# A hybrid decoder block on one core: how the front of its mixers empties its banks, shifts by one token and scales its rows

## The chip, the cores and the metric

One Trainium2 chip; the kernel runs on one of its cores. The metric is the device time of one execution in microseconds (us). Five engines work side by side, each through its own queue of instructions in a fixed order: TensorE (PE in the profile, PEld its weight loads), VectorE (DVE), ScalarE (ACT), GpSimd (POOL) and SyncE (SP), which here only issues DMAs. "ACTq" in a row is a DMA that ACT issues.

## The reference

One decoder layer over 512 tokens of width 1024, all in float32. It has four parts, of which the change touches the first:

```
u = rms_norm(h, norm_mix_g)
z = u @ w_in                                   # 1024 x 3328
o_da = diff_attention(z[:, :1536], ...)        # q, k, v of 512 columns each
o_rw = rwkv7_mix(z[:, 1536:], ...)             # r, k, v of 512 columns, 256 of lora
h = h + concat([o_da, o_rw]) @ w_out
h = h + peer_ffn(rms_norm(h, norm_ffn_g), ...)
h = h + sigmoid(rms_norm(h, norm_ple_g) @ ple_gate_w) * (p @ ple_proj_w)
return rms_norm(h, norm_final_g)
```

And of `rwkv7_mix`, what comes ahead of its recurrence:

```
prev = pad(z_rw[:, :-1], one row of zeros ahead)     # the row of the token before
zs = z_rw + (prev - z_rw) * mu
r, k, v, xw, xa, xg = split(zs)
w = -softplus(-(w0 + tanh(xw) @ w_up)) - 0.5
a = sigmoid(a0 + xa @ a_up);  g = sigmoid(xg) @ g_up
kk = k * k_k;  k = k * (1 + (a - 1) * k_a)
kk = kk / max(norm of kk in each head, 1e-12)
...
y = y + sum(r * k * r_k, over a head) * v
```

The recurrence is computed in chunks of 32 tokens, which needs the keys and the update directions multiplied by running products of the decay and by their inverses.

## The kernel before

Tokens stand on the 128 partitions in four blocks b of 128. Each float32 matmul is done as three in a rounded format: an operand is split into a high half (`hi`, a copy on ACT, L128) and a low half (`lo`, the rest, on DVE, L134), and hi x hi, hi x lo and lo x hi are added in the same bank (L200 to L202). A projection (`proj_steps`, L190) goes over eight k-steps of 128 input columns; in each it does 4 token blocks x 3 matmuls into four banks `acc`, and after the eighth step each block's `consume` empties its bank. The weights arrive by `fetch` on SP in pairs of k-steps (`wraw`, three buffers) and are split with the norm's gain as a scale into `whi` and `wlo`, two buffers of a pair each.

`mixers` (L804) does the front of the two mixers in this order:

- The input's transposed columns `xT` are split pair by pair (`columns`, L830) inside the first projection. The row scales, one over the root mean square of each token, are not applied to the input but to each bank when it is copied out.
- Four projections for the RWKV side, of 512 columns each but for lora's 256: "k", "l" (lora), "r", "v". Their `consume` (in `shift_group`, L403) copies the bank on ACT with the row scale `rs` (L414), then issues two or three DMAs on ACT that write the same tile one row further down (L417, L418, L422: the shift by one token), and then mixes on POOL with three instructions (L423, L424, L426).
- The row scales: POOL squares the columns of `xT` and adds them up (L838, L840, L842), PE adds over partitions with a column of ones (`row_scales`, L847) at k-step 7 of the key group, ACT takes the root (L118), DVE the reciprocal.
- After "r", `rw_keys` (L430) normalises the keys of all four blocks: products on DVE, squares on ACT, a root by Newton steps of small DVE instructions (`rsqrt`, L85).
- `rope_tables` (L319) and `lambdas` (L303) are small work on DVE with Sin and Exp on ACT (L389, L395, L313).
- Then, for each block, `rw_prepare` (L445): tanh and sigmoid of lora's tile on ACT, small matmuls, prefix sums of the decay in each chunk (`pcum` L473, `prem` L480, `ppc` L484), their exponentials (`e_in`, `e_inv`, `e_ex`, `e_end`), the decayed tensors, sixteen transposes (`ptr`, L520), and the products of keys with keys inside a chunk (`psA`, L538). Of the decayed tensors POOL made `bon` (L494, L495), `bh` and `kh` (L504, L505), DVE the others: `aa` x `kk` (L501), and in place `aa` x `e_inv` and `k2` x `e_inv` (L509, L510), which the transposes read.
- Between the steps of `rw_prepare` stand steps of the three projections for attention (q, k, v), of the rope and its transposes (`da_prepare`, L717), as `WEAVE` says, and steps of a small triangular solve (`rw_solve`) in block 2, as `PACE` says.

What follows is not touched: the recurrence and the attention, the out-projection, and then the retrieval with its large streams of weights, which is most of the span.

The order on each engine in this part is not that of the code alone. A scheduler of the framework lists the instructions by its own costs and priorities, pools set when a buffer comes free (`p2` has 28 tiles of 128x512, `p4` 14 of 128x1024), and `behind(i, first)` puts an instruction after another one on its engine without a semaphore. The retrieval's loop and the tail have an order written by hand.

Of the kernel before, what the change touches and what calls it, by code (L numbers as in the profile page):

```python
# [8 lines left out]
F32 = mybir.dt.float32  # L9
# [4 lines left out]
AF = mybir.ActivationFunctionType  # L14
# [39 lines left out]
class Kernel:  # L54
# [248 lines left out]
    def lambdas(self, pool):  # L303
# [9 lines left out]
        nc.scalar.activation(e, e, AF.Exp)  # L313
# [5 lines left out]
    def rope_tables(self, pool, tmp):  # L319
# [69 lines left out]
        nc.scalar.activation(self.sin.rearrange("p b j -> p (b j)"), x0, AF.Sin)  # L389
# [7 lines left out]
    def p2(self, name, shape=(128, 512), dt=F32):  # L397
        return self.pages.tile(list(shape), dt, name=name, tag="p2", bufs=28)
# [4 lines left out]
    def shift_group(self, rs, alloc, g0, n):  # L403
# [7 lines left out]
        def consume(b, ps):  # L411
            z = self.p2("z")
            zt[b] = z
            nc.scalar.activation(z[:, :n], ps, AF.Copy, scale=rs[:, b:b + 1])  # L414
            zp = self.p2("zp")

            nc.scalar.dma_start(zp[1:113, :n], z[0:112, :n])  # L417
            nc.scalar.dma_start(zp[113:128, :n], z[112:127, :n])  # L418
            if b == 0:
                nc.vector.memset(zp[0:1, :n], 0.0)  # L420
            else:
                nc.scalar.dma_start(zp[0:1, :n], zt[b - 1][127:128, :n])  # L422
# [22 lines left out]
    def rw_prepare(self, b, psum, r, k, v, kk, lx, st):  # L445
# [46 lines left out]

        bon = p2("bon")
        nc.gpsimd.tensor_tensor(bon, r, k2, op=OP.mult)  # L494
        nc.gpsimd.tensor_tensor(bon, bon, self.r_k, op=OP.mult)  # L495
        st["bonus"] = sm.tile([128, 8], F32, name="bonus", bufs=NB)
# [6 lines left out]
        bh, kh = p2("bh"), p2("kh")  # L503
        nc.gpsimd.tensor_tensor(bh, aa, e_end, op=OP.mult)  # L504
        nc.gpsimd.tensor_tensor(kh, k2, e_end, op=OP.mult)  # L505
        nc.sync.dma_start(by_row(self.d_bh[b]), bh)
        nc.sync.dma_start(by_row(self.d_kh[b]), kh)
        be, kt = aa, k2
        nc.vector.tensor_mul(be, aa, e_inv)  # L509
        nc.vector.tensor_mul(kt, k2, e_inv)  # L510
# [293 lines left out]
    def mixers(self, ocat_pool, psum):  # L804
# [3 lines left out]
        with ExitStack() as ctx:  # L808
# [17 lines left out]
            ones = cpool.tile([128, 1], F32, name="ones")  # L826
            nc.vector.memset(ones, 1.0)
            xs = {}

            def columns(k):  # L830

                xs[k] = self.p4("xt", [128, 2, T])
                nc.sync.dma_start(xs[k], a["xT"][k * 128:(k + 2) * 128, :].rearrange("(k p) t -> p k t", k=2))
                self.split(hi[:, k:k + 2], lo[:, k:k + 2], xs[k])

            def square(k):
                sq = xs[k]
                nc.gpsimd.tensor_tensor(sq, sq, sq, op=OP.mult)  # L838
                if k:
                    nc.gpsimd.tensor_tensor(xs[0], xs[0], sq, op=OP.add)  # L840
                if k == KC - 2:
                    nc.gpsimd.tensor_tensor(xs[0][:, 0], xs[0][:, 0], xs[0][:, 1], op=OP.add)  # L842

            def row_scales():
                ps = psum.tile([128, NB], F32, name="pss", tag="tp")
                for b in range(NB):
                    nc.tensor.matmul(ps[:, b:b + 1], xs[0][:, 0, b * 128:b * 128 + 128], ones, start=True, stop=True)  # L847
                self.rms(rs, ps)
# [4 lines left out]
            begin = {0: [lambda: columns(2), lambda: square(0)], 2: [lambda: columns(4), lambda: square(2)],  # L853
                     4: [lambda: columns(6), lambda: square(4)], 5: [lambda: square(6)],
                     6: [lambda: self.mixer_consts(cpool)], 7: [row_scales]}
            for tag, c0, n in (("k", 512, 512), ("l", 1536, 256), ("r", 0, 512), ("v", 1024, 512)):
# [6 lines left out]
                if tag == "r":  # L863
                    kks = [self.rw_keys(zs["k"][b]) for b in range(NB)]
# [27 lines left out]
            for b in range(NB):  # L892
                for i, _ in enumerate(self.rw_prepare(b, psum, zs["r"][b], zs["k"][b], zs["v"][b], kks[b], zs["l"][b],
                                                      sts[b])):
# [707 lines left out]
```

## Time and profile before

| | us |
|---|---|
| three runs | 1864.88, 1874.73, 1876.71 |
| their median | 1874.73 |
| the profiled execution | 1859.81 |
| its span in the profile | 1857.4 |

The profile is of one execution: its span runs from the first recorded instruction to the last, and 2.4 us lie around it. Its granted TensorE clock was 0.966 of full speed on the mean. Over the whole span PE was busy 1728.6 us (93%), DVE 1448.7 (78%), ACT 739.5 (40%) and POOL 653.0 (35%). A row of a timeline gives the start of an instruction, its duration, the engine, the line, the operation with the tiles that it writes and reads, and in brackets how long the engine had been idle and what ended that. Buffer numbers are left out of the tiles' names.

### The profile page before, as it was taken

To read this page: it belongs to the slowest core of one execution; us is meant where nothing else is said; L and a number is where in the kernel's file an instruction comes from. 1 tells how busy PE (TensorE), PEld (TensorE's weight loads), DVE (VectorE), ACT (ScalarE), POOL (GpSimd) and SP (SyncE) were. 2 spreads that over 40 slices of the span, in tenths; PEclk is the share of its full clock that TensorE was granted. 3 is DMA by queue.
4 is the path that set the end of the run, shared out by engine and by line. 5 is a ranking of instruction groups with operands and counts; after the bars stand their busy time and mean duration, and the time that the engine had idled before them with its cause. 6 is when DMAs were issued, how large, how long until landed. Compare 5 with 4: busy or idle time off the path is not lost.

```text
span 1857.4 us, 28657 instructions
## 1 busy us (share of the span) xinstructions
PE 1728.6 (93%) x10434; PEld 1465.3 (79%) x10434; DVE 1448.7 (78%) x3233; ACT 739.5 (40%) x1371; POOL 653.0 (35%) x447
## 2 busy tenths in 40 slices
PE   6887987897998987999999999999999999999998
PEld 5755665666777787998777788889899999989886
DVE  6476587667459999987888787887878787878786
ACT  3424342332335654444443433333333333333354
POOL 6662121110126664001111133334545555555530
PEclk9988997889999998999999999999999999999999
DMA  5533224441442343445665678777989898989891
GB/s 171 154 95 97 81 83 91 100 118 34 150 145 83 109 129 100 140 142 192 208 203 201 195 240 272 237 265 274 310 308 310 308 310 305 311 308 313 303 329 65
DMA packets 149842, 361.62 MB, mean 195 GB/s; under 512 B 43859, under 2 KB 58447, under 8 KB 149573
## 3 DMA queue, kind: packets, MB, share of 16 engines
q1 hardware_dynamic: 109924, 221.89, 37.2%
q0 software_dynamic: 36864, 134.23, 21.3%
q10 hardware_dynamic: 2912, 3.67, 0.7%
q8 instruction: 82, 1.34, 0.3%
q14 instruction: 60, 0.48, 0.1%
HBM read 330.51 MB, written 21.36 MB: 189 GB/s over the span
## 4 chain that ended last, share of the span: by engine, by line
PE 68%; DVE 22%; issue 4%; ACT 3%; DMA 1%; POOL 1%; ACTq 0%; SPq 0%; DVEq 0%; POOLq 0%
PE po L1270 21%; PE phid L1134 8%; PE phid L1136 8%; PE phid L1135 8%; PE pg L1239 2%; DVE wlo L132 2%; ACT whi L128 2%; PE acc L201 2%; DVE ids L1083 2%; PE acc L202 2%; PE acc L200 2%; DVE wlo L134 1%; PE psA L538 1%; DVE rest L977 1%; DVE jj L1227 1%
## 5 line engine op out<-in xcount | busy, mean ns | idle before, releaser
L132 DVE TENSOR_TENSOR wlo<-wraw,whi 128x1024 fp32r<-128x1024 f32 x243 | 297.6, 1225 | 150.5 <-ACT whi L128 150.4
L128 ACT ACTIVATE whi<-wraw 128x1024 fp32r<-128x1024 f32 x276 | 291.4, 1057 | 177.7 <-PE phid L1135 59.0
L1136 PE MATMUL phid<-u2dhi,wlo 128*128 128x384 f32 x1024 | 347.7, 340 | 12.7 <-POOL wlo L132 12.7
L1134 PE MATMUL phid<-u2dhi,whi 128*128 128x384 f32 x1024 | 350.9, 343 | 1.0 <-ACT row L1143 1.0
L1135 PE MATMUL phid<-u2dlo,whi 128*128 128x384 f32 x1024 | 346.9, 339 | 0.0
L1293 POOL DMA_INDIRECT row<-in_peer_u_dram,idx x128 | 190.7, 1490 | 404.5 <-DVE row L1305 222.2
L1293 POOL DMA_INDIRECT row<-in_peer_v_dram,idx x128 | 186.1, 1454 | 276.8 <-DVE h L1309 194.8
L1270 PE MATMUL po<-whi,chi 128*128 128x512 f32 x768 | 243.9, 399 | 1.2 <-ACT row L1143 1.2
L1270 PE MATMUL po<-whi,clo 128*128 128x512 f32 x768 | 243.1, 398 | 1.5
L1270 PE MATMUL po<-wlo,chi 128*128 128x512 f32 x768 | 241.4, 395 | 0.0
L1136 PEld LDWEIGHTS phid<-u2dhi,wlo 128*128 128x128 f32 x1024 | 194.7, 190 | 14.8 <-POOL wlo L132 14.8
L1134 PEld LDWEIGHTS phid<-u2dhi,whi 128*128 128x128 f32 x1024 | 194.8, 190 | 5.8 <-ACT row L1143 1.3
L1135 PEld LDWEIGHTS phid<-u2dlo,whi 128*128 128x128 f32 x1024 | 194.4, 190 | 3.7
L1270 PEld LDWEIGHTS po<-whi,clo 128*128 128x128 f32 x768 | 143.0, 188 | 42.0 <-DVE clo L134 8.7
L1270 PEld LDWEIGHTS po<-wlo,chi 128*128 128x128 f32 x768 | 144.4, 188 | 34.3
L1309 DVE SCALAR_TENSOR_TENSOR h<-row,ids,h 128x1024 f32<-128x1024 f32 x128 | 164.0, 1281 | 1.5
L128 ACT ACTIVATE chi<-gelu 128x384 fp32r<-128x384 f32 x128 | 67.4, 526 | 239.8 <-DVE gelu L1247 121.5
L1270 PEld LDWEIGHTS po<-whi,chi 128*128 128x128 f32 x768 | 141.1, 188 | 25.5 <-ACT row L1143 1.5
L1305 DVE SCALAR_TENSOR_TENSOR row<-row,xn 128x1024 f32<-128x1024 f32 x128 | 153.8, 1220 | 0.0
L1143 ACT ACTIVATE gelu<-phid 128x384 f32<-128x384 f32 x86 | 42.3, 492 | 266.9 <-PE phid L1136 266.9
L200 PE MATMUL acc<-whi,uhi 128*128 128x512 f32 (+1 forms) x224 | 91.1, 416 | 18.8 <-ACT whi L128 11.6
L132 POOL TENSOR_TENSOR wlo<-wraw,whi 128x1024 fp32r<-128x1024 f32 x33 | 78.8, 2400 | 68.9 <-ACT whi L128 68.9
(436 smaller groups left out, 2938.0 us busy)
## 6 DMA issues: line engine op xcount, KB each, us to landing
wraw<-in_peer_uT_dram SPq DMA_DIRECT2D x128, 512.0 KB, 3.9
wraw<-in_peer_v_dram SPq DMA_DIRECT2D x128, 512.0 KB, 6.2
wraw<-in_w_in_dram SPq DMA_DIRECT2D x24, 512.0 KB, 6.1
wraw<-in_peer_w_q_dram SPq DMA_DIRECT2D x16, 512.0 KB, 4.4
ahead<-row SPq DMA_DIRECT2D x42, 192.0 KB, 2.3
gelu<-ahead SPq DMA_DIRECT2D x42, 192.0 KB, 3.8
wraw<-in_w_out_dram SPq DMA_DIRECT2D x8, 512.0 KB
zp<-z ACTq DMA_DIRECT2D x12, 224.0 KB, 2.7
```

The costliest lines, as they stand in the source:

```text
L128: self.last_hi = nc.scalar.activation(hi, src, AF.Copy, **({} if g is None else {"scale": g}))
L132: self.last_lo = eng.tensor_tensor(lo, src, hi.bitcast(F32), op=OP.subtract)
L200: nc.tensor.matmul(o, hi[:, k, s], whi, start=(k == 0), stop=False)
L201: nc.tensor.matmul(o, hi[:, k, s], wlo, start=False, stop=False)
L1134: nc.tensor.matmul(ps, whi[:, s], hi[:, k, :], start=(k == 0), stop=False)
L1135: nc.tensor.matmul(ps, whi[:, s], lo[:, k, :], start=False, stop=False)
L1136: nc.tensor.matmul(ps, wlo[:, s], hi[:, k, :], start=False, stop=(k == KC - 1))
L1143: nc.scalar.activation(g, ps, AF.Gelu)
L1270: nc.tensor.matmul(outs[b, e], lhs[:, s], rhs[:, 512 * e:512 * e + 512], start=(c == 0 and rhs is vhi and lhs is chi), stop=(c == NKEY - 1 ...
L1293: nc.gpsimd.indirect_dma_start(out=row, out_offset=None, in_=a["peer_u" if kind == "U" else "peer_v"], in_offset=bass.IndirectOffsetOnAxis ...
L1305: nc.vector.scalar_tensor_tensor(row, row, 1.0, xn0, op0=OP.mult, op1=OP.mult, accum_out=hid0[:, k:k + 1])
L1309: nc.vector.scalar_tensor_tensor(acc0, row, hid0[:, k:k + 1], acc0, op0=OP.mult, op1=OP.add)
```

## The change

The change is in the front of the mixers alone, and its parts are these:

- A projection's four banks are emptied by four copies in a row, and only then come the shifts of the four blocks. The shifts' DMAs are issued by SP instead of ACT.
- The row scales are made from `x` itself: four loads of 128x1024 on SP, and for each a Square on ACT with its sum over the row (`squares`, L111). The squares on POOL and the small matmul on PE are gone.
- Exp of the lambdas and the first Sin are put behind the last bank copy that was issued (`last_z`).
- The keys are normalised block by block, ahead of each `rw_prepare`, instead of all after "r".
- `bon`, `bh` and `kh` are made on DVE instead of POOL, after `be` and `kt`, which now have tiles of their own; the other products go in place.

```diff
 def lambdas
-        nc.scalar.activation(e, e, AF.Exp)
+        self.behind(nc.scalar.activation(e, e, AF.Exp), self.last_z)
 def rope_tables
-        nc.scalar.activation(self.sin.rearrange("p b j -> p (b j)"), x0, AF.Sin)
+        self.behind(nc.scalar.activation(self.sin.rearrange("p b j -> p (b j)"), x0, AF.Sin), self.last_z)
 def shift_group
         def consume(b, ps):
-            z = self.p2("z")
-            zt[b] = z
-            nc.scalar.activation(z[:, :n], ps, AF.Copy, scale=rs[:, b:b + 1])
-            zp = self.p2("zp")
-
-            nc.scalar.dma_start(zp[1:113, :n], z[0:112, :n])
-            nc.scalar.dma_start(zp[113:128, :n], z[112:127, :n])
+            zt[b] = self.p2("z")
+            self.last_z = nc.scalar.activation(zt[b][:, :n], ps, AF.Copy, scale=rs[:, b:b + 1])
+            if b == NB - 1:
+
+                for x in range(NB):
+                    shift(x)
+
+        def shift(b):
+            z, zp = zt[b], self.p2("zp")
+
+            nc.sync.dma_start(zp[1:113, :n], z[0:112, :n])
+            nc.sync.dma_start(zp[113:128, :n], z[112:127, :n])
             if b == 0:
                 nc.vector.memset(zp[0:1, :n], 0.0)
             else:
-                nc.scalar.dma_start(zp[0:1, :n], zt[b - 1][127:128, :n])
+                nc.sync.dma_start(zp[0:1, :n], zt[b - 1][127:128, :n])
 def rw_prepare
-        bon = p2("bon")
-        nc.gpsimd.tensor_tensor(bon, r, k2, op=OP.mult)
-        nc.gpsimd.tensor_tensor(bon, bon, self.r_k, op=OP.mult)
...
         nc.vector.tensor_mul(aa, aa, kk)
         yield
-        bh, kh = p2("bh"), p2("kh")
-        nc.gpsimd.tensor_tensor(bh, aa, e_end, op=OP.mult)
-        nc.gpsimd.tensor_tensor(kh, k2, e_end, op=OP.mult)
+        be, kt = p2("be"), p2("kt")
+        nc.vector.tensor_mul(be, aa, e_inv)
+        nc.vector.tensor_mul(kt, k2, e_inv)
+
+        bon = e_inv
+        nc.vector.tensor_mul(bon, r, k2)
+        nc.vector.tensor_mul(bon, bon, self.r_k)
+        st["bonus"] = sm.tile([128, 8], F32, name="bonus", bufs=NB)
+        bh, kh = aa, k2
+        nc.vector.tensor_mul(bh, aa, e_end)
+        nc.vector.tensor_mul(kh, k2, e_end)
         nc.sync.dma_start(by_row(self.d_bh[b]), bh)
         nc.sync.dma_start(by_row(self.d_kh[b]), kh)
-        be, kt = aa, k2
-        nc.vector.tensor_mul(be, aa, e_inv)
-        nc.vector.tensor_mul(kt, k2, e_inv)
 def mixers
+            ssx = cpool.tile([128, NB], F32, name="ss_mix")
...
-            def square(k):
-                sq = xs[k]
-                nc.gpsimd.tensor_tensor(sq, sq, sq, op=OP.mult)
...
+            def square(b):
+                x = self.p4("xb")
+                nc.sync.dma_start(x, a["x"][b * 128:b * 128 + 128, :])
+                self.squares(x, x, ssx[:, b:b + 1])
 
             def row_scales():
-                ps = psum.tile([128, NB], F32, name="pss", tag="tp")
-                for b in range(NB):
-                    nc.tensor.matmul(ps[:, b:b + 1], xs[0][:, 0, b * 128:b * 128 + 128], ones, start=True, stop=True)
-                self.rms(rs, ps)
+                self.rms(rs, ssx)
...
-            begin = {0: [lambda: columns(2), lambda: square(0)], 2: [lambda: columns(4), lambda: square(2)],
-                     4: [lambda: columns(6), lambda: square(4)], 5: [lambda: square(6)],
-                     6: [lambda: self.mixer_consts(cpool)], 7: [row_scales]}
+            begin = {0: [lambda: columns(2)], 2: [lambda: columns(4)], 4: [lambda: columns(6)],
+                     6: [lambda b=b: square(b) for b in range(NB)] + [lambda: self.mixer_consts(cpool)],
+                     7: [row_scales]}
...
-                if tag == "r":
-                    kks = [self.rw_keys(zs["k"][b]) for b in range(NB)]
...
-                for i, _ in enumerate(self.rw_prepare(b, psum, zs["r"][b], zs["k"][b], zs["v"][b], kks[b], zs["l"][b],
-                                                      sts[b])):
+                for i, _ in enumerate(self.rw_prepare(b, psum, zs["r"][b], zs["k"][b], zs["v"][b],
+                                                      self.rw_keys(zs["k"][b]), zs["l"][b], sts[b])):
```

The scheduler turns this into other orders on every engine; from the out-projection on, the orders of both kernels are the same. Three places follow. A row is the line, the operation, the tiles and the size; "x4" is four in a row.

On ACT, where the key group's banks are emptied, `z<-acc` is a bank's copy, `whi<-wraw` the rounding of a coming weight (128x512 of the key group, 128x256 of lora), `zp<-z` a shift's DMA. Before, from the first bank's copy on:

```order
L414 ACTIVATE z<-acc_126,r_mix 128x512
L128 ACTIVATE whi<-wraw,g_mix 128x256
L417 DMA zp<-z 112x512
L418 DMA zp<-z 15x512
L128 ACTIVATE whi<-wraw,g_mix 128x256
L395 ACTIVATE cos<-x_993 128x32
L414 ACTIVATE z<-acc_127,r_mix 128x512
L422 DMA zp<-z 1x16x32
L417 DMA zp<-z 112x512
L418 DMA zp<-z 15x512
L414 ACTIVATE z<-acc_128,r_mix 128x512
```

Now, from the squares of x on:

```order
L113 ACTIVATE xb,ss_mix<-xb 128x1024 x4
L128 ACTIVATE whi<-wraw,g_mix 128x512
L118 ACT_TABLE_LOAD
L118 ACTIVATE r_mix<-ss_mix,eps 128x4
L128 ACTIVATE whi<-wraw,g_mix 128x256
L413 ACTIVATE z<-acc_125,r_mix 128x512
L413 ACTIVATE z<-acc_126,r_mix 128x512
L413 ACTIVATE z<-acc_127,r_mix 128x512
L128 ACTIVATE whi<-wraw,g_mix 128x256
L413 ACTIVATE z<-acc_128,r_mix 128x512
```

The DMAs and the Cos are gone from between the copies, Exp and Sin from ahead of them, and the squares stand ahead of the key group's last rounding.

On PE, at block 0 of `rw_prepare`, before, from the prefix sums on:

```order
L473 MATMUL pcum<-sw,tri_le 128x512
L480 MATMUL prem<-sw,tri_gt 128x512
L484 MATMUL ppc<-chunk_ind,sw 128x4 x4
L200 MATMUL acc_1106<-whi,uhi 128x512
L201 MATMUL acc_1106<-wlo,uhi 128x512
L202 MATMUL acc_1106<-whi,ulo 128x512
```

There 32 projection matmuls stand between `ppc` and the first of the transposes `ptr`. Now the same place has:

```order
L478 MATMUL pcum<-sw,tri_le 128x512
L485 MATMUL prem<-sw,tri_gt 128x512
L489 MATMUL ppc<-chunk_ind,sw 128x4 x4
L525 MATMUL ptr<-ident,be 128x128 x4
L525 MATMUL ptr<-ident,e_ex 128x128 x4
L525 MATMUL ptr<-ident,e_in 128x128 x4
L525 MATMUL ptr<-ident,kt 128x128 x4
L543 MATMUL psA<-art,beT 128x256 x4
```

No projection matmul is left between the prefix sums and the transposes of block 0; those 32 have moved ahead of the prefix sums or behind the transposes.

On DVE, at the same block, `zs` is the mixed key (and in the row of `e_in` the mixed r), `wlo` a coming weight's low half. Before:

```order
L500 TENSOR_TENSOR e_in<-zs,e_in 128x512
L489 SCALAR_TENSOR_TENSOR ka<-aa,b_rw_k_a 128x512
L498 SCALAR_TENSOR_TENSOR e_ex<-kk,e_ex 128x512
L491 SCALAR_TENSOR_TENSOR zs<-ka,zs 128x512
L501 TENSOR_TENSOR aa<-aa,kk 128x512
L134 SCALAR_TENSOR_TENSOR wlo<-wraw,g_mix,whi 128x512
L512 TENSOR_REDUCE bonus<-bon 128x8
L509 TENSOR_TENSOR aa<-aa,e_inv 128x512
L510 TENSOR_TENSOR zs<-zs,e_inv 128x512
```

Now:

```order
L134 SCALAR_TENSOR_TENSOR wlo<-wraw,g_mix,whi 128x512 x2
L500 TENSOR_TENSOR e_in<-zs,e_in 128x512
L494 SCALAR_TENSOR_TENSOR ka<-aa,b_rw_k_a 128x512
L498 SCALAR_TENSOR_TENSOR e_ex<-kk,e_ex 128x512
L496 SCALAR_TENSOR_TENSOR zs<-ka,zs 128x512
L501 TENSOR_TENSOR aa<-aa,kk 128x512
L504 TENSOR_TENSOR be<-aa,e_inv 128x512
L505 TENSOR_TENSOR kt<-zs,e_inv 128x512
L512 TENSOR_TENSOR aa<-aa,e_end 128x512
L508 TENSOR_TENSOR e_inv<-zs 128x512
L509 TENSOR_TENSOR e_inv<-e_inv,b_rw_r_k 128x512
L513 TENSOR_TENSOR zs<-zs,e_end 128x512
```

The two products that the transposes read stand right behind `aa` x `kk`, and the four that POOL had stand behind these.

## Rows read from the trace of the kernel before

**Rows 1.** Busy time by stretch; start:end, length, PE, PEld, DVE, ACT, POOL (instructions), clock, DMA.

```profile
core 0: us, PE busy (x) PEld busy (x) DVE busy (x) ACT busy (x) POOL busy (x), PEclk, DMA share, GB/s
...
9.50:31.80 22.30, 22.23 (x84) 17.31 (x84) 19.23 (x14) 8.68 (x13) 22.14 (x22) 1.00 0.65 192
31.80:58.30 26.50, 20.60 (x118) 18.26 (x117) 17.12 (x62) 10.33 (x19) 14.00 (x12) 0.81 0.45 131
58.30:112.00 53.70, 48.70 (x201) 36.48 (x199) 24.61 (x39) 21.32 (x38) 31.83 (x27) 1.00 0.43 127
112.00:130.00 18.00, 10.31 (x30) 7.14 (x31) 15.86 (x53) 3.75 (x6) 8.87 (x6) 0.72 0.41 117
130.00:170.50 40.50, 34.48 (x167) 25.78 (x166) 24.17 (x37) 15.06 (x25) 14.82 (x10) 0.96 0.34 102
170.50:210.30 39.80, 32.42 (x161) 23.80 (x162) 20.91 (x54) 16.65 (x27) 6.12 (x8) 0.87 0.25 76
210.30:300.00 89.70, 79.70 (x387) 59.66 (x387) 67.97 (x182) 34.16 (x59) 21.41 (x16) 0.93 0.39 102
...
470.00:1857.00 1387.00, 1340.06 (x7876) 1173.14 (x7874) 1137.41 (x2421) 575.92 (x1055) 512.67 (x324) 0.99 0.67 225
```

**Rows 2.** PE's timeline, key group to lora: start, duration, instruction, [idle before <-what ended it].

```profile
14.85 0.39 PE L200 MATMUL acc<-whi,uhi 128*128 128x512 f32 x1
...
17.64 0.39 PE L200 MATMUL acc<-whi,uhi 128*128 128x512 f32 x1
...
33.78 1.05 PE L847 MATMUL pss<-ones,xt 128*128 128x1 f32 x8 [1.98 <-POOL xt L842]
...
41.48 0.38 PE L200 MATMUL acc<-whi,uhi 128*128 128x256 f32 x1 [2.20 <-ACT z L414]
```

**Rows 3.** ACT's timeline where the key group's banks are emptied.

```profile
37.53 0.20 ACT L313 ACTIVATE lame<-lame 128x2 f32<-128x2 f32 x1 [7.58 <-DVE lams L311]
...
39.05 0.26 ACT L118 ACTIVATE r_mix<-pss,eps 128x4 f32<-128x4 f32 x1
39.33 1.28 ACT L389 ACT_TABLE_LOAD   x1
...
46.22 0.69 ACT L414 ACTIVATE z<-acc,r_mix 128x512 f32<-128x512 f32 x1 [1.50 <-issue]
...
48.39 0.69 ACT L414 ACTIVATE z<-acc,r_mix 128x512 f32<-128x512 f32 x1 [1.48 <-issue]
```

**Rows 4.** Groups of ACT's instructions, the tail's squares: form, count, busy us, mean ns.

```profile
L1414 ACT ACTIVATE sqs<-row 128x1024 f32<-128x1024 f32 x3 | 3.2, 1062 | 0.0
```

**Rows 5.** DVE's timeline, low halves of lora's weights.

```profile
35.40 0.48 DVE L134 SCALAR_TENSOR_TENSOR wlo<-wraw,g_mix,whi 128x256 fp32r<-128x256 f32 x1
...
51.13 9.12 DVE L134 SCALAR_TENSOR_TENSOR wlo<-wraw,g_mix,whi 128x256 fp32r<-128x256 f32 x6 [6.59 <-ACT whi L128]
```

**Rows 6.** PE's timeline from 112 us on, where PE was idle.

```profile
112.52 0.50 PE L200 MATMUL acc<-whi,uhi 128*128 128x512 f32 x1 [1.40 <-ACT z L414]
...
118.77 0.79 PE L201 MATMUL acc<-wlo,uhi 128*128 128x512 f32 x1 [3.48 <-DVE wlo L134]
...
152.00 1.09 PE L520 MATMUL ptr<-ident,aa 128*128 128x128 f32 x4 [4.45 <-DVE aa L509]
...
170.50 0.70 PE L473 MATMUL pcum<-sw,tri_le 128*128 128x512 f32 x1 [0.78 <-ACT sw L466]
...
181.30 1.11 PE L733 MATMUL ptq<-ident,z 128*128 128x128 f32 x4 [4.51 <-DVE z L730]
...
267.44 0.79 PE L201 MATMUL acc<-wlo,uhi 128*128 128x512 f32 x1 [2.70 <-DVE wlo L134]
```

**Rows 7.** Groups of POOL's instructions, 0 to 300 us: the last of three that mix.

```profile
L426 POOL TENSOR_TENSOR zs<-z,zp 128x512 f32<-128x512 f32 x12 | 17.7, 1471 | 0.9
```

**Rows 8.** DMA issues of the page: the shifts; count, KB each, us to landing.

```profile
zp<-z ACTq DMA_DIRECT2D x12, 224.0 KB, 2.7
```

**Rows 9.** DVE's timeline at block 1 of `rw_prepare`.

```profile
175.43 0.69 DVE L501 TENSOR_TENSOR aa<-aa,kk 128x512 f32<-128x512 f32 x1
```

**Rows 10.** Groups of DVE's instructions, 100 to 300 us: a small one of the keys.

```profile
L98 DVE SCALAR_TENSOR_TENSOR knx<-knxi,knx 128x8 f32<-128x8 f32 x12 | 2.7, 245 | 0.0
```

More of the change, by code (lines that the diff above doesn't have):

```diff
@@ L491, in rw_prepare @@
         nc.vector.scalar_tensor_tensor(k2, ka, 1.0, k, op0=OP.add, op1=OP.mult)
-        bon = p2("bon")
-        nc.gpsimd.tensor_tensor(bon, r, k2, op=OP.mult)
-        nc.gpsimd.tensor_tensor(bon, bon, self.r_k, op=OP.mult)
-        st["bonus"] = sm.tile([128, 8], F32, name="bonus", bufs=NB)
         al, rt = e_ex, e_in
@@ L824, in mixers @@
             self.pages = self.pool(ctx, "mx_pages")
-            ones = cpool.tile([128, 1], F32, name="ones")
-            nc.vector.memset(ones, 1.0)
-            xs = {}
+            ssx = cpool.tile([128, NB], F32, name="ss_mix")
             def columns(k):
-                xs[k] = self.p4("xt", [128, 2, T])
-                nc.sync.dma_start(xs[k], a["xT"][k * 128:(k + 2) * 128, :].rearrange("(k p) t -> p k t", k=2))
-                self.split(hi[:, k:k + 2], lo[:, k:k + 2], xs[k])
-            def square(k):
-                sq = xs[k]
-                nc.gpsimd.tensor_tensor(sq, sq, sq, op=OP.mult)
[L839 to L842, printed above, removed]
+                xt = self.p4("xt", [128, 2, T])
+                nc.sync.dma_start(xt, a["xT"][k * 128:(k + 2) * 128, :].rearrange("(k p) t -> p k t", k=2))
+                self.split(hi[:, k:k + 2], lo[:, k:k + 2], xt)
+            def square(b):
+                x = self.p4("xb")
+                nc.sync.dma_start(x, a["x"][b * 128:b * 128 + 128, :])
+                self.squares(x, x, ssx[:, b:b + 1])
             def row_scales():
-                ps = psum.tile([128, NB], F32, name="pss", tag="tp")
-                for b in range(NB):
-                    nc.tensor.matmul(ps[:, b:b + 1], xs[0][:, 0, b * 128:b * 128 + 128], ones, start=True, stop=True)
-                self.rms(rs, ps)
+                self.rms(rs, ssx)
             p2, p4 = self.p2, self.p4
```

## The prediction

> **What bounds the kernel now.** I read the stages first: busy time by stretches, cut where the PE timeline changes from one projection to the next [rows 1]. From 470 us on PE is busy 1340.06 of 1387 us, and the change touches nothing there; the written orders agree from the out-projection on. So all that can move lies ahead of 470, and nearly all of it ahead of 300, in the mixers' front. There PE is the engine with most work, but it idles between stages: 20.60 us busy of 26.5 where the key group ends and the lora group runs, 10.31 of 18.0 from 112 to 130, and the mean granted clock falls with it, to 0.81 and 0.72, so part of these stretches ran at 1.2 GHz instead of 2.4.
>
> Then the PE timeline at those places, for what ended the idle time. A projection matmul of 512 columns starts every 0.2325 us at full clock (twelve from 14.85 to 17.64), so 96 of them, one group of 512, need 22.3 us; one of 256 columns I take at half, 11.2 us for the lora group [rows 2]. The key group's last step waits 1.98 us for POOL's sum of squares, and the lora group starts at 41.48 after another 2.20 us for the first z copy [rows 2]. ACT's timeline says why that copy is late: Exp of the lambdas stands ahead of everything and waits 7.58 us for DVE; behind it a table load, the Sqrt of the row scales at 39.05, another load, and only then z. From there the copies come 2.17 us apart (46.22, 48.39) though one takes 0.69: three shift DMAs are issued on ACT between them, and the next weights' rounding is behind them too [rows 3].
>
> **The change, part by part.** I place each stage with these durations in the order of the changed kernel. Stretch by stretch, before against after:
>
> *31.8 to 58.3 us (k7 and lora), 26.5 us.* Now there is no POOL sum and no small matmul. The four squares take 4 x 1.06 = 4.2 us [rows 4] plus four accumulator reads. They are ahead of the second half of the key group's last weight pair on ACT, and x is fetched ahead of the constants on SP, so they run in ACT's gap from 24 to 29 us. I cost them at nothing; cover is that last weight's slack of about one us, and each us beyond it costs one. The scales are then ready near 31 us, before the first bank is done. Left: 12 matmuls, 2.8 us, and 96 of half width, 11.2. To this I add 4.4 us. DVE prepares a lora weight in 0.48 us alone, but six took 9.12 us beside POOL's mixing, 1.52 each [rows 5]. The first key tile's three mixing instructions now fall into the lora group, beside some forty small instructions of the rope table, and each can hold DVE back by 1.04 (1.52 less 0.48); less half a us of slack, 2.6. The z copies of lora stand behind two roundings of the next group: some 1.8 us. Total 18.4: gain 8.1. Bounds: nothing added, gain 12.5; all eight lora weights at 1.52 and 5 us of rope instructions in line, gain near 5.
>
> *58.3 to 111.1 (r and v), 52.8 us* (111.1 is where the wait of 1.40 before 112.52 begins [rows 6]). Now 2 x 22.3 = 44.6. ACT's tanh and sigmoid of lora stand ahead of v's first weights and wait for POOL, which must mix four key tiles of three instructions of 1.47 us [rows 7] and four lora tiles at half that: 26.5 us from about 37.5, with gaps, since SP issues the shifts between weight fetches that themselves wait for DVE. A shift lands in 2.7 us [rows 8]. I place POOL's end at 71.5, and the first v weights 1.5 us too late. Total 46.1: gain 6.7. If the gaps close there is no wait (8.2); if POOL is 8 us later the gain is gone.
>
> *111.1 to 170.5 (the first attention group and block 0), 59.4 us.* Here PE waited 1.40, 3.48 and more for z copies and for weights that stood on DVE behind the keys of all four blocks [rows 6]. Now the group runs with its 22.3 us, and the block's small first matmuls (2.8 us by my count) move in here. The order then shows nothing between block 0's prefix sums and its transposes, where 32 projection matmuls stood. From pcum to the product that the transposes need: before, in block 1, aa x kk ended 5.6 us after pcum began (170.50 to 176.12) [rows 6, 9], one more multiplication makes 6.3, and two weight splits that stand ahead add 1.5: 7.8 us. Then, as before, 18.5 us from the first transposes at 152.00 to block 1's pcum at 170.50 [rows 6]. Total 51.4: gain 8.0. The wait of 4.45 us ahead of the transposes [rows 6] (aa x e_inv overwrites the aa that POOL's bh reads, and on DVE the sum of POOL's bon stands ahead of it) goes, but the uncovered chain takes its place: here the change gives back what it takes away. Bounds on the chain, 4 to 12 us: gain 4 to 12.
>
> *170.5 to 210.3 (block 1).* PE waited 4.51 us for the rope on DVE after only three projection matmuls; the order now puts 18 there. DVE has the four products that POOL had (4 x 0.69 = 2.8 us [rows 9]) ahead of the rope's end. I take 2.5, between 0 and 4.5.
>
> *210.3 to 300 (blocks 2, 3, the solve).* The wait of 2.70 us behind POOL at 267 goes [rows 6]; DVE gets 2.8 us a block and the keys, three instructions of 0.69 and thirteen small ones of 0.245 [rows 9, 10], 5.3 us: 8.1 a block, while it is already busy 67.97 of 89.7 us [rows 1]. I take 0, between -9 and +6.
>
> The sixteen tiles' shifts cost SP about what they cost ACT, near 1.9 us each by the gaps in rows 3, 30 us in all; SP has nothing else to compute, and the price is in the r and v term.
>
> Sum: 8.1 + 6.7 + 8.0 + 2.5 + 0 = 25.3 us. The profiled execution took 1859.8 us (span 1857.4), so 1834.5; the median of the runs shown is 14.9 us above that execution, and 1874.7 - 25.3 = 1849.4. I say 1850.
>
> **A rule weighed.** Sin, Exp and Sin again now come in a row behind v's copies, three table loads. In the trace the Sqrt of 0.26 us begun at 39.05 ends at 39.31 and the load after it begins at 39.33, so a switch is the 1.28 us of the row and no more [rows 3]; ACT is then free about a us before the next weights are due. The Trainium skill (ScalarE: Activation LUTs, "What ACT_TABLE_LOAD costs") counts a drain of about 1.38 us on top of each load, 2.66 together. The trace doesn't show that drain. By the page ACT would be 4.1 us later there, the next weights some 3 us late, and the sum 22 us, so 1853.
>
> **Rivals.**
> *The shift queue.* The chain SP, shift, POOL, lora's tanh on ACT, v's weights slips by 8 us more. For it: SP's shifts wait in one line behind fetches that wait for DVE, and POOL's 1.47 us a piece is already a contended figure. Against: POOL has nothing else to do there now. PE would lose 8 us and some at 1.2 GHz, 10 in all: 1859.
>
> *The scales late.* 2 MB of x more, where DMA is already busy 0.65 of the stretch [rows 1]. If the squares end 4 us later, the last key weights are late and the clock falls: 7 us, 1857.
>
> *DVE becomes the bound* in blocks 2 and 3: all of 2 x 8.1 us shows, 16, leaving 9: 1866. For it: DVE is full in parts there. Against: PE leads there by 12 us of busy time, and POOL no longer holds DVE back.
>
> *Slower: blocks without cover.* If each of blocks 1 to 3 gets block 0's uncovered chain, PE stands idle about 5 us a block and then does that block's transposes and products at 1.2 GHz, which I put at 8 more: 3 x 13 = 39, so 14 slower than before, 1889. It beats the gain from 8.4 us a block on. Against: the order keeps projections between the steps of these three blocks.
>
> *More than forecast.* The added 4.4 and 1.5 us are not paid and block 1 gives all of 4.5: 33 us and up, near 1840.
>
> **How the numbers follow.** Forecast (1842 to 1858) 0.50; more 0.10; shift queue 0.13; scales late 0.07; DVE bound 0.12; slower 0.08. One per cent is 18.7 us, about what a measurement of this kernel can tell from no change, so faster means below 1856. That takes 0.47 of the forecast's 0.50, all of "more", and 0.09 of the three cases from 1857 to 1866: 0.66. Within: 0.26. Slower: 0.08. The range runs from 1835 to 1873, which leaves out the slower case and the ends of the others.
>
> **What would show it.** Right: lora's matmuls start by 36 us and v's end by 98; no PE wait on z's first copy above 2.5 us; block 0's transposes wait 4 to 6 us, now for the DVE product; block 1's pcum near 148. Wrong: a clock below 0.9 over the lora group; ACT standing at lora's tanh beyond 73 us; DVE busy without a break from 190 to 270 while PE waits for masks or weights; later stages of another length than before.

## The result, and the profile after

The changed kernel takes 1849.2 us (median of 14 runs, 1833.6 to 1864.4); the kernel before, beside it, 1871.65 (14 runs, 1855.3 to 1877.0). The ratio is 0.988, 95% interval 0.985 to 0.991: faster by 1.2%, 22.5 us. The ratio leaves out executions that are more than 1.5% above the fastest of their kernel, here one of the 14 (1864.42 us); the medians here and below are of all.

The two profiled executions hardly differ (1859.81 us before, 1859.97 after). What differs between executions of one kernel is the granted clock. Each one's record has its span and its mean clock c, so the time it spent at the lower level is 2 x (1 - c) x span. Over the 14 of the changed kernel this runs from 99 to 168 us, and the span follows it as 1789.7 + 0.42 x, correlation 0.994. A projection matmul starts every 0.2325 us at the one level [rows 2] and every 0.43 at the other (53.46 to 53.89 below, granted clock 0.50), so a us there does the work of 0.54 and loses 0.46: the slope is near what PE alone would give. I use span - 0.42 x as the "time at the upper clock"; its standard deviation within a kernel is 1 to 3 us, where that of the time is 5 to 10. It is only as good as the one slope: the kernels' own slopes lie between 0.39 and 0.44, but u_pool's is 0.33, so its number is the least certain. Before it is 1803.2 (34 later executions; the 14 beside have only their times on record), after 1790.0: 13 us of the gain are less work or waiting in line. Less time at the lower clock, 135 us against 151, times 0.42, is 7 us more; with 0.7 us less outside the span that is 21 us, near the 22.5 measured.

The stages of the profiled execution, cut as in [rows 1]:

```profile
9.50:31.80 22.30, 22.23 (x84) 17.74 (x85) 9.98 (x13) 13.91 (x22) 0.00 (x0) 1.00 0.84 274
31.80:58.30 26.50, 21.80 (x127) 19.56 (x126) 17.83 (x59) 9.77 (x19) 7.86 (x6) 0.87 0.56 166
58.30:112.00 53.70, 51.16 (x211) 40.27 (x211) 22.27 (x29) 25.00 (x41) 39.01 (x33) 0.97 0.45 134
112.00:130.00 18.00, 16.14 (x70) 12.69 (x68) 11.34 (x11) 5.89 (x10) 11.51 (x9) 1.00 0.56 140
130.00:170.50 40.50, 31.40 (x111) 21.99 (x111) 26.09 (x68) 15.18 (x26) 1.51 (x2) 0.62 0.26 78
170.50:210.30 39.80, 38.50 (x192) 29.46 (x193) 29.49 (x92) 17.75 (x32) 0.84 (x4) 0.96 0.26 74
210.30:300.00 89.70, 76.02 (x424) 54.93 (x422) 72.01 (x214) 32.31 (x59) 11.33 (x10) 0.88 0.40 106
470.00:1858.00 1388.00, 1341.68 (x7866) 1175.83 (x7864) 1136.15 (x2421) 574.10 (x1054) 513.17 (x324) 0.99 0.67 224
```

The hole from 112 to 130 is filled (16.14 busy of 18.0, clock 1.00). A new one stands from 130 to 170.5, at 0.62 of the clock. PE's timeline shows it, against [rows 2, 6]:

```profile
34.80 0.28 PE L200 MATMUL acc<-whi,uhi 128*128 128x256 f32 x1
...
46.62 0.58 PE L201 MATMUL acc<-wlo,uhi 128*128 128x256 f32 x1 [2.92 <-DVE wlo L134]
...
52.74 0.51 PE L200 MATMUL acc<-whi,uhi 128*128 128x512 f32 x1 [1.78 <-ACT z L413]
...
53.46 0.63 PE L202 MATMUL acc<-whi,ulo 128*128 128x512 f32 x1
53.89 0.63 PE L200 MATMUL acc<-whi,uhi 128*128 128x512 f32 x1
...
79.50 0.50 PE L200 MATMUL acc<-whi,uhi 128*128 128x512 f32 x1 [2.54 <-ACT z L413]
...
103.79 0.48 PE L200 MATMUL acc<-whi,uhi 128*128 128x512 f32 x1
...
130.13 1.13 PE L478 MATMUL pcum<-sw,tri_le 128*128 128x512 f32 x2 [1.99 <-ACT sw L471]
...
140.01 1.09 PE L525 MATMUL ptr<-ident,be 128*128 128x128 f32 x4 [7.11 <-DVE be L504]
...
165.02 1.91 PE L478 MATMUL pcum<-sw,tri_le 128*128 128x512 f32 x2
```

Lora starts at 34.80 instead of 41.48, r at 52.7 instead of 58.2, the first attention group at 103.8 instead of 112.5. By block 1's prefix sums at 165.02 (before 170.50) 5.5 us are left. The last projection matmul begins at 277.5 (before 289.4): 11.8 us.

But at the next meeting point, the out-projection's first matmul, only 2.1 us of them are left. PE's timeline before and after, each with the stretch between its two rows (columns as in [rows 1]):

```profile
289.36 0.39 PE L202 MATMUL acc<-whi,ulo 128*128 128x512 f32 x1
...
449.47 0.50 PE L236 MATMUL accr<-whi,ohi 128*128 128x512 f32 x1
...
289.36:449.47 160.11, 134.95 (x1402) 99.19 (x1401) 111.79 (x363) 48.89 (x130) 17.77 (x14) 0.83 0.36 82
```

```profile
277.52 0.39 PE L202 MATMUL acc<-whi,ulo 128*128 128x512 f32 x1
...
447.33 0.50 PE L236 MATMUL accr<-whi,ohi 128*128 128x512 f32 x1
...
277.52:447.33 169.81, 141.39 (x1403) 103.82 (x1401) 113.15 (x363) 48.63 (x130) 17.49 (x14) 0.79 0.35 78
```

The recurrence and the attention, which the change doesn't touch, take 9.7 us longer, with nearly the same order on each engine and a clock of 0.79 instead of 0.83. The kernel before alone differs as much between its two profiles: 160.1 us there and 167.9, at 0.79, in the run again_before below. So one pair of profiles can't show what the change is worth in the time; the many executions do.

### The profile page after: what moved, and what is told of

Read it like the earlier page. It is cut to its first block, busy times and chain, and to the rows that moved or that the text cites. A ratio compares the mean times of both kernels' runs of the same rounds, so it can differ in the third digit from the quotient of the medians.

```text
span 1858.3 us, 28631 instructions
## 1 busy us (share of the span) xinstructions
PE 1742.4 (94%) x10426; PEld 1479.2 (80%) x10426; DVE 1436.7 (77%) x3248; ACT 746.6 (40%) x1382; POOL 605.7 (33%) x423
## 4 chain that ended last, share of the span: by engine, by line
PE 65%; DVE 19%; issue 3%; ACT 3%; DMA 1%; POOL 0%; SPq 0%; DVEq 0%; ACTq 0%; POOLq 0%
PE po L1265 21%; PE phid L1129 8%; PE phid L1131 8%; PE phid L1130 8%; PE pg L1234 2%; DVE wlo L132 2%; DVE ids L1078 1%; PE psA L543 1%; ACT whi L128 1%; DVE rest L972 1%; DVE jj L1222 1%; PE psS L758 1%; DVE si L970 1%; DVE si L974 1%; DVE gelu L1242 1%
## 5 line engine op out<-in xcount | busy, mean ns | idle before, releaser
L1265 PEld LDWEIGHTS po<-whi,chi 128*128 128x128 f32 x768 | 141.4, 189 | 25.3 <-ACT row L1138 1.5
```

The costliest lines, as they stand in the source:

```text
L1265: nc.tensor.matmul(outs[b, e], lhs[:, s], rhs[:, 512 * e:512 * e + 512], start=(c == 0 and rhs is vhi and lhs is chi), stop=(c == NKEY - 1 ...
```

## The experiments

All runs stand in one table. The interval is that of the ratio to the kernel before on the same chip. "Upper" is the mean time at the upper clock, "lower" the median time at the lower level, both from the spans and clocks of the executions. The first row is the kernel before beside again_before, again_after, w5_cover0 and w4_cover0; beside u_pool, u_p1, u_scales and u_keys it is 1870.0 (29 executions), 1802.8 and 153, beside o_p5, x_pool, after_early and p1_early 1869.4 (28), 1801.8 and 153.

| run | median us (n) | ratio, 95% | upper | lower |
|---|---|---|---|---|
| the kernel before | 1870.6 (34) | | 1803.2 | 151 |
| again_before | 1869.4 (12) | 0.9995, 0.996 to 1.003 | 1802.4 | 151 |
| again_after | 1849.9 (11) | 0.990, 0.987 to 0.994 | 1789.5 | 137 |
| u_pool | 1868.0 (12) | 1.001, 0.998 to 1.004 | 1795.0 | 172 |
| o_p5 | 1853.2 (11) | 0.991, 0.988 to 0.995 | 1792.5 | 141 |
| x_pool | 1872.3 (12) | 1.003, 1.000 to 1.006 | 1800.3 | 165 |
| u_p1 | 1844.5 (6) | 0.989, 0.984 to 0.994 | 1791.1 | 123 |
| u_scales | 1853.7 (12) | 0.991, 0.988 to 0.995 | 1787.1 | 156 |
| u_keys | 1853.5 (12) | 0.992, 0.989 to 0.995 | 1791.7 | 139 |
| w5_cover0 | 1855.2 (12) | 0.995, 0.992 to 0.998 | 1787.6 | 157 |
| w4_cover0 | 1866.9 (12) | 1.000, 0.997 to 1.003 | 1792.7 | 173 |
| after_early | 1846.8 (12) | 0.988, 0.985 to 0.992 | 1788.5 | 135 |
| p1_early | 1848.8 (6) | 0.990, 0.985 to 0.994 | 1790.0 | 133 |

**Both kernels once more.** No edit.

> The changed kernel as it is, once more. Theory: the profile of the changed kernel fell into one of its executions with the least clock (0.956, where its 14 runs reach from 0.955 to 0.973), so that the front's gain in it is too small: here lora still starts at 34 to 36 us, v still ends at 100 to 104 (neither depends much on the clock), but block 0's transposes to block 1's pcum takes 18 to 22 us instead of 25.0, and the last projection matmul of the mixers ends at 265 to 275 us instead of 277.5. Rival: the low clock after block 0 belongs to the kernel, since PE idles there every time: 25 us again, and 277.5 within 2 us. Median 1840 to 1855 by both.

> The kernel before as it is, once more. Theory: its profile fell into one of its quick executions (1859.8 us where the median of 14 is 1871.7), so here the time is 1862 to 1877, and the last projection matmul of the mixers ends later than 289.3 us, at 290 to 300. Rival: the front takes the same time in each execution, 289.3 within 2 us, and what varies lies behind it. Ratio 1.0 within its interval by both.

In the second profile of the changed kernel block 0's transposes to block 1's pcum take 25.2 us again, and 22 of them are at the lower clock; the last projection matmul begins at 282.9. The rival held for the hole, not for its "277.5 within 2 us". But the theory was hardly put to the test: this execution has a clock of 0.952, the first profile's 0.956, and the 25 executions of the two runs reach 0.973. Whether one with a higher clock has the hole too is not shown. The kernel before has its last projection matmul at 292.0, as its theory said. So the front gains 11.8 us in one pair of profiles and 9.0 in the other; at the out-projection's first matmul (459.9 and 454.2 in this pair) 2.1 and 5.7 are left.

**Cover for block 0's chain.** The edit is one number row: two (w5: four steps ahead, then two, two) or three (w4) steps of the attention projections after block 0's first parts.

```diff
-WEAVE = (0, (1, 1, 1, 1, 1, 1, 0, 0), ...
+WEAVE = (4, (2, 2, 1, 1, 1, 1, 0, 0), ...     # w5_cover0
+WEAVE = (0, (3, 3, 3, 2, 1, 1, 0, 0), ...     # w4_cover0
```

> The changed kernel with four steps of the first attention group ahead of block 0 and two steps after each of its first two parts, so that projection matmuls stand between block 0's prefix sums and its products again. Theory: block 0's uncovered chain (7.1 us of waiting, then 20 us at the lower clock) is the change's own loss; here PE waits under 2 us at block 0's transposes, and the last projection matmul of the mixers ends 6 to 10 us earlier than in the changed kernel's run beside it, the median 5 to 12 us lower, so about 1838 to 1845 and a ratio near 0.982. Rival: the projections that are moved ahead are missing as cover later (block 3 has none in the order): the front ends within 3 us of the changed kernel, median within 4 us of it.

> The changed kernel with three steps of projections after each of block 0's first three parts and two after the fourth: all of the first attention group still stands ahead of block 0, and the second group's matmuls stand between its prefix sums and its products. Theory: as with the other kernel of this kind, PE waits under 2 us more at the transposes than the copies of the first group cost, and the front ends 5 to 10 us earlier than the changed kernel's, median 1838 to 1846. Rival: within 4 us of the changed kernel, since the second group's rope now stands on DVE ahead of block 0's products and cover is missing in block 3.

In w5 the wait ahead of the transposes is gone from PE's timeline:

```profile
147.02 0.60 PE L525 MATMUL ptr<-ident,be 128*128 128x128 f32 x4
...
251.95 1.09 PE L525 MATMUL ptr<-ident,be 128*128 128x128 f32 x4 [7.90 <-DVE be L504]
```

At the upper clock it wins 2 us on again_after, but it spends some 20 us more at the lower one, and is 5 us slower; w4 is 17 us slower. Theory wrong in the time: a stretch without PE work is moved, not filled. In w5 the last projection matmul begins at 240.8, ahead of block 3's transposes, and there (the second row) PE waits 7.90 us; from 235.9 to 280 its clock is 0.64.

**The products on POOL again** (the last part undone, be and kt staying as they are):

```diff
-        bon = e_inv
-        nc.vector.tensor_mul(bon, r, k2)
-        nc.vector.tensor_mul(bon, bon, self.r_k)
+        bon = p2("bon")
+        nc.gpsimd.tensor_tensor(bon, r, k2, op=OP.mult)
+        nc.gpsimd.tensor_tensor(bon, bon, self.r_k, op=OP.mult)
...
-        bh, kh = aa, k2
-        nc.vector.tensor_mul(bh, aa, e_end)
-        nc.vector.tensor_mul(kh, k2, e_end)
+        bh, kh = p2("bh"), p2("kh")
+        nc.gpsimd.tensor_tensor(bh, aa, e_end, op=OP.mult)
+        nc.gpsimd.tensor_tensor(kh, k2, e_end, op=OP.mult)
```

> The changed kernel with bon, bh and kh on POOL again, in tiles of their own, be and kt staying first and in tiles of their own on DVE. Theory: with be and kt in their own tiles nothing on PE's path waits for POOL any more, and DVE loses 2.8 us a block: 1787 to 1791 at the upper clock, no slower than the changed kernel. Rival: POOL and DVE hold each other back (POOL's products at 1.3 us and more, DVE's at up to twice their 0.69), and moving them to DVE was worth 3 us or more: 1793 or more.

The theory fell, and by far: the whole gain in the time is gone, 5 us of it at the upper clock and the rest by 37 us more at the lower one (172 against 135). The groups of DVE and of POOL, 125 to 300 us, show the price; the columns are count, busy us, mean ns and idle time before. u_pool, then the changed kernel:

```profile
L505 DVE TENSOR_TENSOR kt<-zs,e_inv 128x512 f32<-128x512 f32 x4 | 7.0, 1762 | 0.0
L504 DVE TENSOR_TENSOR be<-aa,e_inv 128x512 f32<-128x512 f32 x4 | 5.8, 1439 | 0.1
...
L512 POOL TENSOR_TENSOR bh<-aa,e_end 128x512 f32<-128x512 f32 x4 | 6.2, 1542 | 0.0
```

```profile
L504 DVE TENSOR_TENSOR be<-aa,e_inv 128x512 f32<-128x512 f32 x4 | 2.8, 689 | 0.1
...
L505 DVE TENSOR_TENSOR kt<-zs,e_inv 128x512 f32<-128x512 f32 x4 | 2.7, 686 | 0.0
```

The same products take 0.69 us on DVE in the changed kernel, and 1.44 and 1.76 on the mean in u_pool, where POOL works beside them. But the scheduler also makes another order around POOL's products, so this run alone does not tell sharing from order.

**The products alone, and POOL's work alone.** o_p5 is the kernel before with the same part of the diff and nothing else. x_pool is the changed kernel with POOL products whose results nobody reads, and with PE's, DVE's, ACT's and SP's orders unchanged:

```diff
+        for _ in range(2):
+            idle = p2("idle")
+            nc.gpsimd.tensor_tensor(idle, r, e_end, op=OP.mult)
+            nc.gpsimd.tensor_tensor(idle, idle, self.r_k, op=OP.mult)
         bh, kh = aa, k2
```

> The kernel before with the last part of the change alone: be and kt in tiles of their own, bon, bh and kh after them on DVE. New theory, after the changed kernel with these products on POOL lost all that it had gained (1868.0): these products are the change, and the other four parts are worth next to nothing together in the time, since what they win ahead of 111 us is lost again by block 1. Then the time is 1848 to 1856 and 1790 to 1794 at the upper clock. Rival: the parts only work together (the products can leave POOL with profit only where the banks are emptied in a row and keys come block by block), and alone this one gives 1860 to 1870.

> The changed kernel with four more products of 128x512 on POOL in each block, which read the mixed r and the decay to the chunk's end and write tiles that nobody reads; the order of PE, DVE, ACT and SP is the same. Theory: POOL's products cost by holding back DVE while both work (be took 1.71 us beside bon and bh in block 2 where it takes 0.69 alone), so that this kernel loses as well: 1793 to 1797 at the upper clock, 1858 to 1868 us. Rival: it is not the sharing but the order that the scheduler makes around POOL's products, and the waits for them; then nothing here waits for POOL, and the time is that of the changed kernel within 4 us, 1789 to 1791 at the upper clock.

o_p5's theory held. So did that of x_pool in its sign, beyond its numbers: 1800.3 at the upper clock, 10.8 more than the same kernel without these products (again_after), and 28 us more at the lower clock. DVE's timeline in block 1 of x_pool, while POOL is busy from 174.64 on:

```profile
174.37 0.69 DVE L498 SCALAR_TENSOR_TENSOR e_ex<-kk,e_ex 128x512 f32<-128x512 f32 x1
174.97 1.77 DVE L496 SCALAR_TENSOR_TENSOR zs<-ka,zs 128x512 f32<-128x512 f32 x1
176.66 1.76 DVE L501 TENSOR_TENSOR aa<-aa,kk 128x512 f32<-128x512 f32 x1
178.34 1.30 DVE L734 TENSOR_TENSOR ropem<-z,cos 128x64 f32<-128x64 f32 x1
```

A product of 0.69 takes 1.76, a rope step of 64 columns 1.30; the others of its kind in this kernel take 0.22. Blocks 1 to 3, from block 1's pcum to the last chunk product, as one stretch (columns as in [rows 1]); the kernel before, the changed one, x_pool and o_p5:

```profile
170.50:285.60 115.10, 100.47 (x497) 74.71 (x497) 82.31 (x204) 45.35 (x76) 25.09 (x22) 0.93 0.28 84
```

```profile
164.80:274.00 109.20, 102.93 (x499) 75.16 (x498) 88.43 (x263) 45.99 (x78) 7.13 (x10) 0.93 0.29 83
```

```profile
168.70:292.50 123.80, 107.41 (x499) 78.78 (x498) 101.05 (x263) 46.06 (x78) 28.21 (x22) 0.90 0.25 74
```

```profile
167.40:277.20 109.80, 105.18 (x496) 76.41 (x495) 79.15 (x217) 45.17 (x76) 7.17 (x10) 0.90 0.28 81
```

With the same 263 instructions DVE is busy 101.05 us instead of 88.43 once POOL has 21 us more to do. And o_p5 has thirteen DVE instructions more than the kernel before in 3 us less of busy time. Waiting for POOL is not the cause in x_pool: from 125 to 300 us one wait alone is put down to the unread products (ACT's copy `beT` of block 0, 5.15 us), and that copy starts 1.17 us after the first transpose, in the changed kernel 1.18. So x_pool shows that POOL's products cost the time through DVE. It does not show that all of o_p5's 16 us is this: o_p5 also gives be and kt tiles of their own. But u_pool has these tiles too, with the products on POOL, and gains nothing in the time.

**The other parts undone, one at a time.** u_p1: each bank's shifts right behind its copy, on ACT. u_scales: squares on POOL, sum on PE. u_keys: all keys after r. Each is the corresponding piece of the change's diff, backwards; Exp and Sin were not tried alone.

> The changed kernel with its first part undone: each bank's shifts are issued by ACT right behind that bank's copy again, the next copy after them. All numbers 'at the upper clock' are a run's span less 0.42 us for each us that it spent at the lower clock, 2 x (1 - granted clock) x span; 0.42 is the slope over the 14 runs of the changed kernel, which come to 1790.0 with a spread of 1.0, the kernel before to 1803. Theory: copies in a row are worth 4 to 7 us at the upper clock (1794 to 1797), with copies 2.2 us apart and PE waiting at the first and second bank of lora; POOL mixes earlier, so lora's tanh no longer holds ACT up and v's start is not late, which gives some of it back. Rival: what matters is only how soon POOL mixes, and the kernel is as fast or faster without this part: 1790 or less.

> The changed kernel with the row scales made as before: squares of the transposed columns on POOL, sum over partitions on PE at the key group's step 7. Theory: step 7 waits 2 us for POOL again, the root is ready later than the first bank, lora starts at 38 to 40 us instead of 34.6, and that stays: 1793 to 1796 at the upper clock. Rival: the gain at lora's start came from Exp and Sin having left ACT's queue, not from the scales: lora at 36 us or earlier, 1790 to 1792.

> The changed kernel with the keys of all four blocks normalised after the r group, as before. Theory: block 0's prefix sums no longer wait for a square and block 0's chain on DVE is 3 to 4 us shorter, but the keys hold back weights on DVE in the first attention group as they did before (waits of 2 to 4 us): 1788 to 1793 at the upper clock. Rival: the delay of weights was the main loss of the kernel before, so that this part is most of the change's gain: 1796 or more.

At the start u_p1 and u_scales do what was expected. u_p1's PE waits for banks in lora:

```profile
40.94 0.39 PE L200 MATMUL acc<-whi,uhi 128*128 128x256 f32 x1 [2.07 <-ACT z L414]
44.04 0.39 PE L200 MATMUL acc<-whi,uhi 128*128 128x256 f32 x1 [1.46 <-ACT z L414]
...
130.41 2.08 PE L473 MATMUL pcum<-sw,tri_le 128*128 128x512 f32 x2 [9.90 <-ACT sw L466]
```

and u_scales has the wait for the sum back, lora starting at 40.4:

```profile
33.72 1.55 PE L852 MATMUL pss<-ones,xt 128*128 128x1 f32 x8 [2.45 <-POOL xt L847]
```

In u_keys block 0's prefix sums wait for nothing, as expected, but they come at 136.4, 6 us later than in the changed kernel.

In the end none of the three differs from the changed kernel by more than the intervals: 1844.5, 1853.7 and 1853.5 beside 1849.2. At the upper clock copies in a row are worth 1 us, not 4 to 7; keys block by block 2; the scales from x cost 3 rather than win 3, while u_scales spends 20 us more at the lower clock. The theories of u_p1 and u_scales were off: they let an early gain stand. That of u_keys held in its number (1791.7, inside 1788 to 1793).

**Two waits of the changed kernel taken away** (tanh behind v's fourth weight, block 0's keys after r), on it and on u_p1:

```diff
+                among = {3: [lambda: setattr(self, "mark", self.last_hi)]} if tag == "v" else {} if zs else begin
...
+                if tag == "r":
+                    kk0 = self.rw_keys(zs["k"][0])
```

> The changed kernel with lora's tanh and sigmoid behind the v group's fourth weight instead of r's last one, and block 0's keys right after the r group. Theory: ACT no longer stands at the tanh until POOL is through (77.2 us), so PE doesn't wait 2.5 us ahead of the v group, v ends 3 to 4 us earlier; block 0's prefix sums come without a square ahead of them and PE waits 3 to 4 us at the transposes instead of 7.1. Together 5 to 8 us at the upper clock, 1782 to 1785, and less time at the lower clock: 1836 to 1845 us. Rival: what is won ahead of block 1 is lost by the mixers' end, as in the other runs: 1788 to 1790 and 1846 to 1853.

> The same two moves on the changed kernel with shifts issued by ACT behind each bank's copy (1844.5 alone, where PE waited 9.9 us for block 0's prefix sums behind a square of the keys). Theory: that wait goes to 3 us or less, and this is the fastest of all: 1785 to 1788 at the upper clock, 1832 to 1841 us. Rival: no more than the one without them, 1842 to 1847.

In after_early v's last matmul begins at 93.5 us, ten earlier, and then PE stands at the next group's weights:

```profile
106.94 1.22 PE L200 MATMUL acc<-whi,uhi 128*128 128x512 f32 x2 [5.34 <-ACT whi L128]
```

4 us are left at block 0's pcum, 6 at the last projection matmul (271.5), 1.5 at the upper clock in the end. after_early's rival held in both numbers; p1_early is no faster than u_p1, as its rival said, but 2 us above the rival's range. No version beats the changed kernel beyond its interval.

## Why the prediction was right or wrong

The time and the sign were right: 1850 said, 1849.2 measured, inside 1842 to 1858. The reasons were mostly not, and that the number came out so close is luck in good part. The sum put 22.8 of its 25.3 us on the stretches up to block 1's pcum, that is mostly on banks, scales, shifts and keys; 5.5 were measured there. u_pool has these four parts and its products on POOL: 1868.0 against 1870.0 beside it, nothing in the time. By the upper column they win 8 us (1802.8 to 1795.0), which 19 us more at the lower clock take back. The last part alone is o_p5: 16 us of the 22.

Of the prediction's own signs, lora by 36 came; v's end by 98 (its last matmul begins at 103.3), a wait of 4 to 6 us at block 0's transposes (7.11) and block 1's pcum near 148 (165.0) did not. Two signs of being wrong came: ACT at lora's tanh beyond 73 us, and later stages of another length.

- *k7 and lora, gain 8.1.* Anchor right (34.8, "by 36"), no sum on POOL, scales at 30.9. The weights' slack was mis-sized: a lora weight waited 2.92 us on DVE behind rope instructions, and 5.5 us were gained, near the lower bound of 5.
- *r and v, gain 6.7.* "I place POOL's end at 71.5": it was 77.2. The shift queue was the rival, and it came with 5.7 of its 8 us. SP's timeline shows it, then POOL's:

```profile
47.43 0.46 SPq L82 DMA_DIRECT2D b_rw_ln_g<-in_rw_ln_g_dram  x1
52.72 0.37 SPq L158 DMA_DIRECT2D wraw<-in_w_in_dram  x1
53.14 0.56 SPq L422 DMA_DIRECT2D zp<-z  x1
```

```profile
58.31 1.28 POOL L428 TENSOR_TENSOR zp<-zp,z 128x512 f32<-128x512 f32 x1 [6.97 <-DMA zp<-z]
...
76.43 0.73 POOL L431 TENSOR_TENSOR zsl<-z,zp 128x256 f32<-128x256 f32 x1
```

  The third key tile's shift stands behind a weight fetch that goes out at 52.72, and POOL waits 6.97 us. ACT stands at lora's tanh until 77.19, so r's banks are copied late and PE waits 2.54 us at 79.50. From r's first matmul to the attention group's it took 51.1 us, not 46.1 (before, 54.2).
- *First attention group and block 0, gain 8.0.* "The uncovered chain takes its place" was right (7.11 us of waiting, 4 to 6 said), but not "then, as before, 18.5 us": it was 25.0, since the clock fell during that wait and stayed at the lower level for most of the block (0.62 on the mean from 130 to 170.5). From the group's start to block 1's pcum 61.2 us, before 58.0: a loss of 3. I had priced low clock after an uncovered chain only in the rival for blocks 1 to 3, not in block 0 where the order showed the chain.
- *Block 1, gain 2.5; blocks 2 and 3, 0.* Sizes near: 4.1 and 2.3 us (pcum to pcum 35.6 against 39.7; on to the last projection matmul 76.9 against 79.2). The reason failed: "DVE gets ... 8.1 a block" took 0.69 us for a product from a row that began while POOL was idle [rows 9], and left out what DVE gets back. The kernel before had its own price beside POOL, and it was not looked up (its groups of DVE, 125 to 300 us):

```profile
L509 DVE TENSOR_TENSOR aa<-aa,e_inv 128x512 f32<-128x512 f32 x4 | 5.9, 1478 | 0.5 <-POOL bh L504 0.5
L510 DVE TENSOR_TENSOR zs<-zs,e_inv 128x512 f32<-128x512 f32 x4 | 4.9, 1218 | 0.0
```

  So moving a product from POOL costs DVE 0.69 and gives back up to 1.07 for each product it ran beside. The prediction had priced this for lora's weights (1.04 us for each mixing instruction), but for the products it stands only as a word against a rival ("POOL no longer holds DVE back"), without a price. The Trainium skill (SBUF — State Buffer, "Who interferes with whom") says that a DVE instruction with two inputs in SBUF contends with a GpSimd instruction that reads SBUF, and calls the ports that the two share an exclusive lock. x_pool agrees: beside POOL's instructions of 1.5 to 1.6 us a product of 0.69 becomes 1.76 and a rope step of 0.22 becomes 1.30, both 1.1 us more. That rule spoke for the change, and it was the one to weigh.
- *The rule that was weighed* doesn't show here either: behind v's copies, which end at 104.44, come three switches, each load within 0.04 us of the instruction before it and of its use. The first two:

```profile
101.65 2.79 ACT L413 ACTIVATE z<-acc,r_mix 128x512 f32<-128x512 f32 x4 [2.16 <-PE acc L202]
104.45 1.28 ACT L389 ACT_TABLE_LOAD   x1
105.74 0.23 ACT L389 ACTIVATE sin<-x 128x32 f32<-128x32 f32 x1
105.99 1.28 ACT L313 ACT_TABLE_LOAD   x1
```

The front of the profiles gained 9 to 12 us, half of the sum or less, and 2 to 6 of them reach the out-projection. The time gained 22: 13 us at the upper clock, and 7 because the typical execution after spends 16 us less at the lower clock, for which the sum had no term of its own. The base was off as well: the median of three that it started from, 1874.73, is 3 us above that of 14. Why one order of much the same work spends 123 us at the lower clock (u_p1) and another 173 (w4_cover0) is left open: u_pool has 172, more than the kernel before, with the same products on POOL.

## What to carry to other kernels

Take an instruction's duration from rows where its neighbours are as they will be: a product on POOL is not free because POOL would be idle; here DVE paid for it. An early gain is not a gain until a later meeting point shows it; the four parts that in u_pool start lora 7.3 us earlier than before (34.16) and the attention group 10.5 earlier (102.02) were worth next to nothing in the time. Where executions differ by their granted clock, take span against time at the lower level first: it brought a range of 31 us down to 3.5 for the changed kernel, and showed what single pairs of profiles hid.

## What the runs showed of the hardware that was not expected

Products on POOL that nobody reads, in an order otherwise the same, cost 22 us of 1850 (x_pool against again_after), though they keep POOL busy only 21 us more in blocks 1 to 3. And the time of one kernel is nearly a straight line in its time at the lower clock: 0.42 us for each us over 14 executions of the changed kernel, correlation 0.994 (0.91 to 0.99 in the other runs), which leaves little of its spread to other causes. The stretch behind the change, from the last projection matmul to the out-projection, took 160.1 us at a mean clock of 0.83 in one profile of the kernel before and 167.9 at 0.79 in the other; in the changed kernel 169.8 at 0.79 and 171.3 at 0.78.
